# A gathered mixture of experts: 1280 dense and 768 gathered value columns from two table copies, sums in PSUM, 256 low parts on GpSimd

## The chip, the cores and the metric

The kernel runs on one core of one Trainium2 chip. The metric is the device time of one execution in microseconds. An execution has five engines that work side by side: TensorE (PE, with its weight loads as PEld), VectorE (DVE), ScalarE (ACT), GpSimd (POOL) and SyncE (SP, which here only issues transfers). Each runs its own instructions in order and waits for the others by semaphores.

## The reference, cut to what matters

The program is one decoder block over 256 tokens of width 2048. Its last part, which the change is about, is a mixture of experts: each token picks 16 of 16384 experts in each of 8 heads, weighs them, and sums their rows of the value table.

```python
def peer_ffn(y, wq, sub_keys, u_tab, v_tab):
    ...
        u = u_tab[eidx]                                   # 256 tokens, 8 heads, 16 experts, 2048 columns
        v = v_tab[eidx]
        h = jax.nn.gelu(jnp.einsum('btd,bthkd->bthk', yb, u))
        return jnp.einsum('bthk,bthkd->btd', g * h, v).astype(y.dtype)
...
        ffn = peer_ffn(x, peer_wq[l], peer_keys[l], peer_u[l], peer_v[l])
        x = layer_norm(DN_ALPHA * x + ffn, ln2_g[l], ln2_b[l])
```

Both tables have 16384 rows of 2048 columns in float32.

## The kernel before, in words

The program runs in stages: input projections, attention and convolution, output projection and the first layer norm, then the U stage (a score for each token and expert, about 425 to 870 us), a stage that turns scores into weights, the V stage (about 1080 to 1575 us), and the second layer norm. The change is in the V stage, in what leads into it and in the last norm.

The V stage sums the value rows in two ways, by column. For the columns from `GC` = 640 on (`VC` = 1408 of them) the sum is dense: the 16384 rows are taken in 128 steps of 128 rows, and in each step TensorE multiplies the weights `W` of both halves of the tokens (tt 0 and 1, 128 tokens each) with the 128 rows. For the first 640 columns it is gathered: token p of half tt has 128 chosen experts; in step j GpSimd issues an indirect transfer that brings the row of the j-th choice of each token, and VectorE adds it, times its weight `wv`, to `gacc`.

TensorE multiplies in three products per block, since one pass rounds: `mm3` takes high part times high part (L296), high times low (L297) and low times high (L298). ACT rounds the 128 x 1408 tile `vr` to its high part `vh` (L1785), VectorE subtracts to get the low part `vl` (L1786), and so for the weights, `wh` and `wl`, for two steps at once (L1774, L1775). The 1408 columns are three blocks of 512, 512 and 384, so a step has 18 matmuls: three blocks, two halves, three products. Their sums stay in six PSUM tiles (`f`) from the first step to the last.

The order is written out by hand, with no scheduler. In step j the loop issues the load and the gathers of step j+2 (`v_load`: SP for `vr`, POOL for `gv`), splits the rows of step j+1 (`v_split`), adds the gathered rows of step j (`v_gather`), and multiplies step j (`v_use`). `vr` has three buffers, `gv` has `GVB` = 7, and `vh` and `vl` have one in each of two pools that alternate, so the split of step j+1 overwrites what the matmuls of step j-1 read. Nine of the 256 gathers, the entries of `AHEAD`, are made before the stage begins: ACT scales them by their weight (L1799) and GpSimd adds them to `gacc` (L1802), between other work; 247 sums over 125 steps are left (L1750). The last three steps have no gathers. Step 0's split is made ahead too, by GpSimd.

In the U stage the same kinds of work appear: the dense table rows come from a copy that the host lays out contiguously (`u_dense`), GpSimd issues gathers `gu` (L1168), VectorE's dot products read a token row `yp` that lies in PSUM (L1179), and the low part `ul` is shared between VectorE (L1237) and GpSimd (L1238). The `hp` matmuls there (L1515, L1516, L1519) have 256 columns. In the projections L257 makes low parts of 512 columns on VectorE and GpSimd after one ACT instruction.

After step 127 the second layer norm runs block by block: `L2066` adds the residual `z` of half 1 by a matmul, `L2104` that of half 0 on VectorE, then statistics (L2097), `center` (L2089) and `shift` (L2093) on VectorE; one block of half 0 and the gathered columns of both halves go over ACT (L2083) and GpSimd (L2084, L2085).

Of the kernel before, what the change touches and what calls it, by code (L numbers as in the profile page):

```python
# [1 line left out]

# [6 lines left out]
F32 = mybir.dt.float32  # L9
# [4 lines left out]
AF = mybir.ActivationFunctionType  # L14
OP = mybir.AluOpType
# [4 lines left out]
P = 128  # L20
# [14 lines left out]
BIG = 1.0e33  # L35
GC = 640
AHEAD = (*range(9, 100, 12), 126)
LATER = {9: (125, 0), 33: (126, 1), 45: (127, 0), 69: (125, 1), 93: (127, 1)}
GVB = 7
UG = 896  # L40
# [6 lines left out]
VC = D - GC  # L47
# [32 lines left out]
def tile_hybrid_block(  # L80
    ctx: ExitStack,
    tc: tile.TileContext,
    x, w_in, pos_k, w1_k, w2_k, pos_v, w1_v, w2_v, dw_w, dw_b, cln_g, cln_b,
    w_out, ln1_g, ln1_b, wq, keys, u_dense, u_rows, v_tab, ln2_g, ln2_b, out,
    dbg=None, stop=None,
):
    nc = tc.nc
    x, w_in, w_out, wq = x[0], w_in[0], w_out[0], wq[0]
    v_tab, out = v_tab[0], out[0]
    dbg = dbg or {}  # L90
# [1646 lines left out]
    def v_raw(j):  # L1737
        raws[j] = vr_.tile([P, VC], F32, name=f"vr{j}", tag="vr", bufs=3)
        nc.sync.dma_start(raws[j], v_tab[j * P:(j + 1) * P, GC:])

    gvs = {}

    def v_fetch(j, tt):
        gvs[j, tt] = vr_.tile([P, GC], F32, name=f"gv{j}_{tt}", tag="gv", bufs=GVB)
        nc.gpsimd.indirect_dma_start(  # L1745
            out=gvs[j, tt], out_offset=None, in_=v_tab,
            in_offset=bass.IndirectOffsetOnAxis(ap=fl(e4, tt)[:, j:j + 1], axis=0))

    def v_sum(j, tt, engine):
        engine.scalar_tensor_tensor(gacc[:, tt], gvs.pop((j, tt)), wv[:, tt, j:j + 1], gacc[:, tt],  # L1750
                                    op0=OP.mult, op1=OP.add)
# [25 lines left out]
    def v_cols(j, s, early=False):  # L1777
# [6 lines left out]
        else:  # L1784
            nc.scalar.activation(vh, src[:, s], AF.Copy)  # L1785
        (nc.gpsimd if early else nc.vector).tensor_tensor(vl, src[:, s], vh.bitcast(F32), op=OP.subtract)  # L1786

# [195 lines left out]
    if stop == "u":  # L1983
        dump("hv", hv)
        if "H" in dbg:
# [5 lines left out]
    vps.append(vp_)  # L1991
    acc = [[psv_.tile([P, 512], F32, name=f"f{tt}{b}", tag=f"f{tt}{b}")[:, :e - a]
            for b, (a, e) in enumerate(blocks)]
           for tt in range(2)]

    def v_gather(j):
# [3 lines left out]
    def v_part(j, tt, b, stop=False):  # L2000
        (wh, wl), vhl = halves_[j // 2], parts[j]
        (a, e), s = blocks[b], slice(tt * P, tt * P + P)
        mm3(acc[tt][b], wh[:, s, j % 2], wl[:, s, j % 2], vhl[0][:, a:e], vhl[1][:, a:e], j == 0, stop)

# [14 lines left out]
    z2 = []  # L2019
    if True:  # L2020
        v_rows(0, 1)
        for j in range(P):
# [3 lines left out]
            if j == 0:  # L2026
                pass
            elif j + 2 < P:
# [22 lines left out]
            if j == P - 3:  # L2051
                for tt in range(2):
                    for i in range(2):
                        nc.vector.bn_stats(stat[:, tt, nb + i], gacc[:, tt, i * GC // 2:(i + 1) * GC // 2])
            if j == 0:
# [6 lines left out]

        for tt in range(2):
            if tt:
                for b, (a, e) in enumerate(blocks):
                    nc.tensor.matmul(acc[tt][b], lhsT=scaled, rhs=z2[tt][:, a:e], start=False, stop=False)  # L2066
            for j in (P - 2, P - 1):
                for b in range(nb):
                    v_part(j, tt, b, j == P - 1)
        zb = [acc[tt] + [gacc[:, tt]] for tt in range(2)]  # L2070
        zs = [[z2[tt][:, a:e] for a, e in blocks] + [gacc[:, tt]] for tt in range(2)]
# [60 lines left out]
        "dw_w", "dw_b", "conv_ln_g", "conv_ln_b", "w_out", "ln1_g", "ln1_b",  # L2132
        "peer_wq", "peer_keys", "peer_u_dense", "peer_u_rows", "peer_v", "ln2_g", "ln2_b"]
_OUTS = [((1, T, D), "float32")]
# [27 lines left out]
```

## Time and profile before

| what | value |
|---|---|
| median of 3 runs | 1589.48 us (1586.29 to 1589.81) |
| the profiled execution | 1588.19 us, its span 1586.4 us |
| busy: PE, DVE, ACT, POOL | 1550.8, 1367.0, 899.4, 1044.3 us |
| granted TensorE clock | 0.993 |
| bytes read from HBM | 459.80 MB, 293 GB/s over the span |

A group's row reads: line, engine, operation, the tile written `<-` the tiles read, the shape written `<-` the shape read, how many; then busy microseconds and mean nanoseconds of one; then the engine's idle time just before them and what ended most of it. A row of the timeline begins with its start and its length in microseconds, and `xN` marks merged instructions. A row of the windows gives each engine's busy time, the granted clock, the mean busy share of the 16 DMA engines and the GB/s that they moved. A row of the DMA queues gives packets, MB and the share of time that the packets took; q1 carries SP's loads, q0 GpSimd's gathers. Matmuls are pipelined and overlap, so the distance between two starts tells what one costs, not its length.

### The profile page before, as it was taken

The page shows a single profiled execution, that of the slowest core. Times are in us where ns is not written, and L with a number is a line of the kernel's source. Part 1 is how long each engine was busy: PE and PEld are TensorE (multiplying, and loading weights), DVE is VectorE, ACT ScalarE, POOL GpSimd, SP SyncE. Part 2 cuts the span into 40 slices and gives each one's busy share as a digit, 9 for nine tenths or more (in the row PEclk, how much of TensorE's full clock was granted, in tenths as well). Part 3 has the DMA queues.
Part 4 walks back from the last instruction along what each step waited for, and adds up shares of the span by engine and source line. Part 5 has one row for each costly group of instructions (what it writes and reads, how often), then busy time and mean ns, then how long its engine had stood idle before and what let it go on. Part 6 is the DMA issues. An engine that isn't in the chain of part 4 may idle for free.

```text
span 1586.4 us, 29450 instructions
## 1 busy us (share of the span) xinstructions
PE 1550.8 (98%) x10987; PEld 1435.9 (91%) x10987; DVE 1367.0 (86%) x2509; ACT 899.4 (57%) x1266; POOL 1044.3 (66%) x791
## 2 busy tenths in 40 slices
PE   9999999999999999999998999999999999999997
PEld 9999999988999999999998977788888888888886
DVE  6999777766578999999997788888999989989998
ACT  5345776645435777777776656785444444444443
POOL 1886000064887777777776677867888878878883
PEclk9999999999999999999999999999999999999999
DMA  9774455255867999999999886767999999999997
GB/s 299 239 231 147 139 161 184 92 207 182 258 209 272 397 382 393 383 390 384 387 388 366 304 276 216 235 196 247 346 368 355 356 371 346 357 376 355 366 356 248
DMA packets 161896, 466.59 MB, mean 294 GB/s; under 512 B 18304, under 2 KB 86424, under 8 KB 161496
## 3 DMA queue, kind: packets, MB, share of 16 engines
q1 hardware_dynamic: 117188, 261.95, 47.8%
q0 software_dynamic: 41040, 201.82, 34.5%
q8 instruction: 86, 1.41, 0.4%
q10 hardware_dynamic: 3524, 0.95, 0.3%
q14 instruction: 58, 0.48, 0.1%
HBM read 459.80 MB, written 4.85 MB: 293 GB/s over the span
## 4 chain that ended last, share of the span: by engine, by line
PE 83%; DVE 7%; DMA 3%; POOL 3%; issue 2%; ACT 2%; POOLq 0%; ACTq 0%; DVEq 0%
PE f L297 10%; PE f L298 10%; PE f L296 10%; PE hp L1515 8%; PE hp L1516 8%; PE hp L1519 7%; PE bank L1722 3%; DVE taps L492 2%; PE pwq L298 2%; PE pwq L297 2%; PE pwq L296 2%; PE bank L1674 2%; DMA feat<-fr 1%; PE mixa L296 1%; PE pcg L297 1%
## 5 line engine op out<-in xcount | busy, mean ns | idle before, releaser
L1745 POOL DMA_INDIRECT gv<-in_peer_v_dram,e x256 | 400.5, 1565 | 91.1 <-DVE gacc L1750 48.3
L1785 ACT ACTIVATE vh<-vr 128x1408 fp32r<-128x1408 f32 (+1 forms) x129 | 175.8, 1364 | 274.8 <-DVE gacc L1750 230.9
L297 PE MATMUL f<-vl,wh 128*128 128x512 f32 (+1 forms) x768 | 288.3, 375 | 1.7 <-DVE vl L1786 1.7
L296 PE MATMUL f<-vh,wh 128*128 128x512 f32 (+1 forms) x768 | 288.5, 376 | 0.0
L298 PE MATMUL f<-vh,wl 128*128 128x512 f32 (+1 forms) x768 | 288.1, 375 | 0.0
L1515 PE MATMUL hp<-yh,uh 128*128 128x256 f32 x1152 | 283.8, 285 | 4.2 <-ACT W L1522 4.2
L1516 PE MATMUL hp<-yl,uh 128*128 128x256 f32 x1152 | 283.4, 284 | 0.0
L257 POOL TENSOR_TENSOR lo<-raw,hi 128x1024 fp32r<-128x1024 f32 (+1 forms) x84 | 189.0, 2271 | 133.9 <-ACT hi L239 127.8
L1168 POOL DMA_INDIRECT gu<-in_peer_u_rows_dram,e x200 | 193.6, 968 | 117.9 <-DVE gu L1179 72.0
L1786 DVE TENSOR_TENSOR vl<-vr,vh 128x1408 fp32r<-128x1408 f32 (+1 forms) x129 | 206.5, 1602 | 41.3 <-ACT vh L1785 39.9
L1515 PEld LDWEIGHTS hp<-yh,uh 128*128 128x128 f32 x1152 | 222.5, 193 | 4.8 <-ACT W L1522 4.8
L1516 PEld LDWEIGHTS hp<-yl,uh 128*128 128x128 f32 x1152 | 222.6, 193 | 0.0
L1179 DVE SCALAR_TENSOR_TENSOR gu<-gu,yp 128x896 f32<-128x896 f32 x200 | 211.2, 1080 | 12.2 <-DMA gu<-in_peer_u_rows_dram,e 12.2
L239 ACT ACTIVATE hi<-raw 128x1024 fp32r<-128x1024 f32 (+1 forms) x137 | 141.2, 1036 | 141.0 <-PE pcg L297 29.1
L1750 DVE SCALAR_TENSOR_TENSOR gacc<-gv,hv,gacc 128x640 f32<-128x640 f32 x247 | 207.4, 880 | 2.9 <-DMA gv<-in_peer_v_dram,e 2.8
L1232 ACT ACTIVATE uh<-ur 128x1152 fp32r<-128x1152 f32 x128 | 149.6, 1168 | 95.6 <-issue 69.3
L297 PEld LDWEIGHTS f<-vl,wh 128*128 128x128 f32 x768 | 148.8, 194 | 22.9 <-DVE vl L1786 2.4
L296 PEld LDWEIGHTS f<-vh,wh 128*128 128x128 f32 x768 | 148.8, 194 | 20.7
L298 PEld LDWEIGHTS f<-vh,wl 128*128 128x128 f32 x768 | 149.0, 194 | 19.5
L1519 PE MATMUL hp<-yh,ul 128*128 128x256 f32 x1152 | 159.3, 284 | 0.0
L1519 PEld LDWEIGHTS hp<-yh,ul 128*128 128x128 f32 x1152 | 147.6, 192 | 0.1
L1237 DVE TENSOR_TENSOR ul<-ut,uh 128x768 fp32r<-128x768 f32 x126 | 119.9, 952 | 26.1 <-ACT ut L1236 23.2
(407 smaller groups left out, 3491.6 us busy)
## 6 DMA issues: line engine op xcount, KB each, us to landing
vr<-in_peer_v_dram SPq DMA_DIRECT2D x128, 704.0 KB
ur<-in_peer_u_dense_dram SPq DMA_DIRECT2D x128, 576.0 KB
raw<-in_w_in_dram SPq DMA_DIRECT2D x32, 1024.0 KB
raw<-in_w_out_dram SPq DMA_DIRECT2D x16, 1024.0 KB
raw<-in_peer_wq_dram SPq DMA_DIRECT2D x15, 1024.0 KB
gv<-in_peer_v_dram,e POOLq DMA_INDIRECT x256, 7.4
gu<-in_peer_u_rows_dram,e POOLq DMA_INDIRECT x200, 6.5
raw<-in_w_in_dram SPq DMA_DIRECT2D x4, 608.0 KB
```

Source lines behind the costliest of these rows:

```text
L257: e.tensor_tensor(lo[:, a:b], src[:, a:b], hi[:, a:b].bitcast(F32), op=OP.subtract)
L296: nc.tensor.matmul(acc, lhsT=ah, rhs=bh, start=start, stop=False)
L297: nc.tensor.matmul(acc, lhsT=ah, rhs=bl, start=False, stop=False)
L298: nc.tensor.matmul(acc, lhsT=al, rhs=bh, start=False, stop=stop)
L1168: nc.gpsimd.indirect_dma_start(out=gt, out_offset=None, in_=u_rows, in_offset=bass.IndirectOffsetOnAxis(ap=fl(e4, tt)[:, c:c + 1], axis=0))
L1179: nc.vector.scalar_tensor_tensor(gt, gt, 1.0, yr, op0=OP.mult, op1=OP.mult, accum_out=hv[:, tt, c:c + 1])
L1515: nc.tensor.matmul(hps[j], lhsT=uh[:, s], rhs=chunk(yh, k), start=k == 0, stop=False)
L1516: nc.tensor.matmul(hps[j], lhsT=uh[:, s], rhs=chunk(yl, k), start=False, stop=False)
L1519: nc.tensor.matmul(hps[j], lhsT=ul[:, s], rhs=chunk(yh, k), start=False, stop=k == UK - 1)
L1745: nc.gpsimd.indirect_dma_start(out=gvs[j, tt], out_offset=None, in_=v_tab, in_offset=bass.IndirectOffsetOnAxis(ap=fl(e4, tt)[:, j:j + 1], ...
L1750: engine.scalar_tensor_tensor(gacc[:, tt], gvs.pop((j, tt)), wv[:, tt, j:j + 1], gacc[:, tt], op0=OP.mult, op1=OP.add)
L1786: (nc.gpsimd if early else nc.vector).tensor_tensor(vl, src[:, s], vh.bitcast(F32), op=OP.subtract)
```

## The change

`GC` becomes 768 and so `VC` 1280: blocks of 512, 512 and 256. The host hands over two copies of the value table, `v_dense` with the last 1280 columns and `v_rows_` with the first 768, each contiguous. The gathered sums go to `pg`, a PSUM tile of three banks, to which ACT copies `gacc` ahead of the split for step 1; the two 256-column accumulators share one bank, `fboth`. For a whole step VectorE makes the low part of 1024 columns and GpSimd that of the other 256. The gather ring has six buffers and, from the second gather of step 3 on, two more in another pool for every fourth gather. The last multiplications come in another order, so that the shared bank is done before the last two blocks of half 1. Lines after the change are two or more further down: L298 to L300 are the three products, L1749 the gather, L1754 the sum, L1789 and L1794 the high and low parts.

```diff
@@ -1,4 +1,5 @@
 from contextlib import ExitStack
+from itertools import count
 
 import concourse.bass as bass
 import concourse.tile as tile
@@ -33,10 +34,11 @@
 ALPHA = 2.0 ** 0.25
 NEG = -3.0e38
 BIG = 1.0e33
-GC = 640
+GC = 768
 AHEAD = (*range(9, 100, 12), 126)
 LATER = {9: (125, 0), 33: (126, 1), 45: (127, 0), 69: (125, 1), 93: (127, 1)}
-GVB = 7
+GVB = 6
+GVX = 2
 UG = 896
 UD = D - UG
 UK = UD // P
@@ -81,12 +83,12 @@
     ctx: ExitStack,
     tc: tile.TileContext,
     x, w_in, pos_k, w1_k, w2_k, pos_v, w1_v, w2_v, dw_w, dw_b, cln_g, cln_b,
-    w_out, ln1_g, ln1_b, wq, keys, u_dense, u_rows, v_tab, ln2_g, ln2_b, out,
+    w_out, ln1_g, ln1_b, wq, keys, u_dense, u_rows, v_dense, v_rows_, ln2_g, ln2_b, out,
     dbg=None, stop=None,
 ):
     nc = tc.nc
     x, w_in, w_out, wq = x[0], w_in[0], w_out[0], wq[0]
-    v_tab, out = v_tab[0], out[0]
+    out = out[0]
     dbg = dbg or {}
 
     def dump(name, ap):
@@ -1736,18 +1738,20 @@
 
     def v_raw(j):
         raws[j] = vr_.tile([P, VC], F32, name=f"vr{j}", tag="vr", bufs=3)
-        nc.sync.dma_start(raws[j], v_tab[j * P:(j + 1) * P, GC:])
-
-    gvs = {}
+        nc.sync.dma_start(raws[j], v_dense[j * P:(j + 1) * P])
+
+    gvs, gv_turns = {}, count()
 
     def v_fetch(j, tt):
-        gvs[j, tt] = vr_.tile([P, GC], F32, name=f"gv{j}_{tt}", tag="gv", bufs=GVB)
+        turn = next(gv_turns) if len(vps) > 1 else 0
+        pool, bufs = (vps[1], GVX) if turn % (GVB // GVX + 1) == 1 else (vr_, GVB)
+        gvs[j, tt] = pool.tile([P, GC], F32, name=f"gv{j}_{tt}", tag="gv", bufs=bufs)
         nc.gpsimd.indirect_dma_start(
-            out=gvs[j, tt], out_offset=None, in_=v_tab,
+            out=gvs[j, tt], out_offset=None, in_=v_rows_,
             in_offset=bass.IndirectOffsetOnAxis(ap=fl(e4, tt)[:, j:j + 1], axis=0))
 
     def v_sum(j, tt, engine):
-        engine.scalar_tensor_tensor(gacc[:, tt], gvs.pop((j, tt)), wv[:, tt, j:j + 1], gacc[:, tt],
+        engine.scalar_tensor_tensor(pg[:, tt], gvs.pop((j, tt)), wv[:, tt, j:j + 1], pg[:, tt],
                                     op0=OP.mult, op1=OP.add)
 
     def v_rest(j):
@@ -1783,7 +1787,11 @@
             nc.gpsimd.tensor_copy(vh, src[:, s])
         else:
             nc.scalar.activation(vh, src[:, s], AF.Copy)
-        (nc.gpsimd if early else nc.vector).tensor_tensor(vl, src[:, s], vh.bitcast(F32), op=OP.subtract)
+        whole = s == slice(0, VC)
+        for e, c in ((nc.vector, slice(0, 1024)), (nc.gpsimd, slice(1024, VC))) if whole else \
+                ((nc.gpsimd if early else nc.vector, s),):
+            vh, vl = (t[:, c] for t in vhl)
+            e.tensor_tensor(vl, src[:, c], vh.bitcast(F32), op=OP.subtract)
 
     def v_split(j):
         if j % 2 == 0:
@@ -1989,9 +1997,12 @@
     psv_ = psv.enter_context(tc.tile_pool(name="psv", bufs=1, space=PSUM, reuse_waits="tile"))
     vp_ = psv.enter_context(tc.tile_pool(name="vp1", bufs=1, reuse_waits="tile", side="right"))
     vps.append(vp_)
-    acc = [[psv_.tile([P, 512], F32, name=f"f{tt}{b}", tag=f"f{tt}{b}")[:, :e - a]
-            for b, (a, e) in enumerate(blocks)]
+    acc = [[psv_.tile([P, 512], F32, name=f"f{tt}{b}", tag=f"f{tt}{b}") for b in range(nb - 1)]
            for tt in range(2)]
+    both = flat3(psv_.tile([P, 512], F32, name="fboth", tag="fboth"), 2, VC - blocks[-1][0])
+    for tt in range(2):
+        acc[tt].append(both[:, tt])
+    pg = psv_.tile([P, 2, GC], F32, name="pg", tag="pg")
 
     def v_gather(j):
         for pair in v_rest(j):
@@ -2000,7 +2011,8 @@
     def v_part(j, tt, b, stop=False):
         (wh, wl), vhl = halves_[j // 2], parts[j]
         (a, e), s = blocks[b], slice(tt * P, tt * P + P)
-        mm3(acc[tt][b], wh[:, s, j % 2], wl[:, s, j % 2], vhl[0][:, a:e], vhl[1][:, a:e], j == 0, stop)
+        mm3(acc[tt][b], wh[:, s, j % 2], wl[:, s, j % 2], vhl[0][:, a:e], vhl[1][:, a:e],
+            j == 0 and not (tt and b == nb - 1), stop)
 
     def v_use(j, tts=range(2)):
         for b in range(nb):
@@ -2024,7 +2036,8 @@
                 v_split(2)
                 v_gather(0)
             if j == 0:
-                pass
+                for tt in range(2):
+                    nc.scalar.activation(pg[:, tt], gacc[:, tt], AF.Copy)
             elif j + 2 < P:
                 v_load(j + 2)
             elif len(z2) < 2:
@@ -2051,7 +2064,7 @@
             if j == P - 3:
                 for tt in range(2):
                     for i in range(2):
-                        nc.vector.bn_stats(stat[:, tt, nb + i], gacc[:, tt, i * GC // 2:(i + 1) * GC // 2])
+                        nc.vector.bn_stats(stat[:, tt, nb + i], pg[:, tt, i * GC // 2:(i + 1) * GC // 2])
             if j == 0:
                 v_use(j, (0,))
                 v_use(j, (1,))
@@ -2060,14 +2073,22 @@
         for b, (a, e) in enumerate(blocks):
             nc.sync.dma_start(bcol[b], ln2_b[:, GC + a:GC + e].to_broadcast([P, e - a]))
 
-        for tt in range(2):
-            if tt:
-                for b, (a, e) in enumerate(blocks):
-                    nc.tensor.matmul(acc[tt][b], lhsT=scaled, rhs=z2[tt][:, a:e], start=False, stop=False)
-            for j in (P - 2, P - 1):
-                for b in range(nb):
-                    v_part(j, tt, b, j == P - 1)
-        zb = [acc[tt] + [gacc[:, tt]] for tt in range(2)]
+        def residual(b):
+            a, e = blocks[b]
+            nc.tensor.matmul(acc[1][b], lhsT=scaled, rhs=z2[1][:, a:e], start=False, stop=False)
+
+        for j in (P - 2, P - 1):
+            for b in range(nb):
+                v_part(j, 0, b, j == P - 1 and b < nb - 1)
+        residual(nb - 1)
+        for j in (P - 2, P - 1):
+            v_part(j, 1, nb - 1, j == P - 1)
+        for b in range(nb - 1):
+            residual(b)
+        for j in (P - 2, P - 1):
+            for b in range(nb - 1):
+                v_part(j, 1, b, j == P - 1)
+        zb = [acc[tt] + [pg[:, tt]] for tt in range(2)]
         zs = [[z2[tt][:, a:e] for a, e in blocks] + [gacc[:, tt]] for tt in range(2)]
 
 
@@ -2130,7 +2151,7 @@
 
 _INS = ["x", "w_in", "cmp_pos_k", "cmp_w1_k", "cmp_w2_k", "cmp_pos_v", "cmp_w1_v", "cmp_w2_v",
         "dw_w", "dw_b", "conv_ln_g", "conv_ln_b", "w_out", "ln1_g", "ln1_b",
-        "peer_wq", "peer_keys", "peer_u_dense", "peer_u_rows", "peer_v", "ln2_g", "ln2_b"]
+        "peer_wq", "peer_keys", "peer_u_dense", "peer_u_rows", "peer_v_dense", "peer_v_rows", "ln2_g", "ln2_b"]
 _OUTS = [((1, T, D), "float32")]
 
 
@@ -2147,6 +2168,8 @@
     u = inputs["peer_u"][0]
     inputs["peer_u_dense"] = u[:, :UD].reshape(P, P, UK, P).transpose(0, 3, 2, 1).reshape(P * P, UD)
     inputs["peer_u_rows"] = u[:, UD:]
+    v = inputs["peer_v"][0]
+    inputs["peer_v_dense"], inputs["peer_v_rows"] = v[:, GC:], v[:, :GC]
     for name in _INS:
         a = _np.ascontiguousarray(inputs[name])
         arrays[f"in_{name}_dram"] = a
```

VectorE's queue in two steps of the V stage, before and after. `hv` is the name that the tile of the weights `wv` bears there.

```order
L1775 TENSOR_TENSOR wl_17024<-W,wh_17023 128x512 [waits PE_49,Activation_49]
L1786 TENSOR_TENSOR vl_17028<-vr_16987,vh_17027 128x1408 [waits DMAHW5_49,Activation_49]
L1750 SCALAR_TENSOR_TENSOR gacc<-gv_0_16955,hv,gacc 128x640 [waits DMASW5_49,DVE_49]
L1750 SCALAR_TENSOR_TENSOR gacc<-gv_1_16957,hv,gacc 128x640 [waits DMASW6_49,DVE_49]
L1786 TENSOR_TENSOR vl_17058<-vr_17017,vh_17057 128x1408 [waits DMAHW6_49,Activation_49]
```

```order
L1779 TENSOR_TENSOR wl_17075<-W,wh_17074 128x512 [waits PE_49,Activation_49]
L1794 TENSOR_TENSOR vl_17079<-vr_17037,vh_17078 128x1024 [waits DMAHW3_49,Activation_49]
L1754 SCALAR_TENSOR_TENSOR pg<-gv_0_17004,hv,pg 128x768 [waits DMASW1_49,DVE_49]
L1754 SCALAR_TENSOR_TENSOR pg<-gv_1_17006,hv,pg 128x768 [waits DMASW2_49,DVE_49]
L1794 TENSOR_TENSOR vl_17110<-vr_17068,vh_17109 128x1024 [waits DMAHW4_49,Activation_49]
```

The order is the same; the low part is 384 columns shorter, the sums are 128 wider, and they read and write `pg`.

GpSimd's queue in the same stage, before and after (the waits name the ring of transfers, DMASW, and the engine that frees a buffer; `e` holds the row numbers).

```order
L1745 DMA gv_0_16861<-in_peer_v_dram,e_4315 128x640 [waits DMASW0_49,DVE_49]
L1745 DMA gv_1_16863<-in_peer_v_dram,e_4315 128x640 [waits DMASW1_49,DVE_49]
L1745 DMA gv_0_16891<-in_peer_v_dram,e_4315 128x640 [waits DMASW2_49,DVE_49]
L1745 DMA gv_1_16893<-in_peer_v_dram,e_4315 128x640 [waits DMASW3_49,DVE_49]
L1745 DMA gv_0_16925<-in_peer_v_dram,e_4315 128x640 [waits DMASW4_49,DVE_49]
```

```order
L1794 TENSOR_TENSOR vl_16846<-vr_16804,vh_16845 128x256 [waits DMAHW4_49,Activation_49]
L1749 DMA gv_0_16872<-in_peer_v_rows_dram,e_4315 128x768 [waits DMASW1_49,DVE_49]
L1749 DMA gv_1_16874<-in_peer_v_rows_dram,e_4315 128x768 [waits DMASW2_49,DVE_49]
L1794 TENSOR_TENSOR vl_16881<-vr_16839,vh_16880 128x256 [waits DMAHW5_49,Activation_49]
L1749 DMA gv_0_16907<-in_peer_v_rows_dram,e_4315 128x768 [waits DMASW3_49,DVE_49]
L1749 DMA gv_1_16909<-in_peer_v_rows_dram,e_4315 128x768 [waits DMASW4_49,DVE_49]
L1794 TENSOR_TENSOR vl_16912<-vr_16870,vh_16911 128x256 [waits DMAHW6_49,Activation_49]
```

Between the gathers of step j+2 and those of j+3 now stands a subtraction that waits for ACT's high part of step j+1.

ACT's queue where the V stage begins, before and after.

```order
L1774 ACTIVATE wh_13228<-W 128x256 [waits DVE_49,Activation_49]
L1785 ACTIVATE vh_13352<-vr_12956 128x1408 [waits DMAHW6_49,DMAHW5_49,DMAHW7_49,DMAHW4_49,DMAHW2_49]
L1774 ACTIVATE wh_13374<-W 128x512 [waits DMAHW4_49,DMAHW5_49,DMAHW3_49,DMAHW6_49,DMAHW2_49,DMAHW7_49,DMAHW1_49,DMAHW0_49]
L1785 ACTIVATE vh_13378<-vr_13226 128x1408 [waits DMAHW2_49,PE_49,Pool_49]
L2050 ACTIVATE scaled<-ident 128x128
```

```order
L1778 ACTIVATE wh_13228<-W 128x256 [waits DVE_49,Activation_49]
L2040 ACTIVATE pg<-gacc 128x768 [waits PE_49,Pool_49]
L2040 ACTIVATE pg<-gacc 128x768 [waits Activation_49]
L1789 ACTIVATE vh_13354<-vr_12956 128x1280 [waits DMAHW6_49,DMAHW7_49,DMAHW5_49,DMAHW2_49]
L1778 ACTIVATE wh_13377<-W 128x512 [waits DMAHW6_49,DMAHW4_49,DMAHW7_49,DMAHW1_49,DMAHW0_49]
L1789 ACTIVATE vh_13381<-vr_13226 128x1280 [waits DMAHW2_49,PE_49]
L2063 ACTIVATE scaled<-ident 128x128
```

Two copies from `gacc` to `pg` have come in front of the high part for step 1; the first of them waits for GpSimd and for TensorE.

TensorE's last matmuls of a step and the first of the next, before and after.

```order
L296 MATMUL f_13340<-vh_16161,wh_16127 128x384
L297 MATMUL f_13340<-vl_16162,wh_16127 128x384
L298 MATMUL f_13340<-vh_16161,wl_16128 128x384
L296 MATMUL f_13343<-vh_16161,wh_16127 128x384
L297 MATMUL f_13343<-vl_16162,wh_16127 128x384
L298 MATMUL f_13343<-vh_16161,wl_16128 128x384
L296 MATMUL f_13338<-vh_16195,wh_16191 128x512 [waits Activation_49]
L297 MATMUL f_13338<-vl_16196,wh_16191 128x512 [waits DVE_49]
```

```order
L298 MATMUL fboth<-vh_13852,wh_13848 128x256
L299 MATMUL fboth<-vl_13853,wh_13848 128x256 [waits Pool_49]
L300 MATMUL fboth<-vh_13852,wl_13849 128x256
L298 MATMUL fboth<-vh_13852,wh_13848 128x256
L299 MATMUL fboth<-vl_13853,wh_13848 128x256
L300 MATMUL fboth<-vh_13852,wl_13849 128x256
L298 MATMUL f_13338<-vh_13883,wh_13848 128x512 [waits Activation_49]
L299 MATMUL f_13338<-vl_13884,wh_13848 128x512 [waits DVE_49]
```

The third block writes one bank for both halves, and its first high-times-low product waits for GpSimd.

## The prediction

> **What bounds the kernel now.** I read the page's chain first, then the groups by shape and one step of the timeline, to see what paces the V stage; then the windows and DMA queues, to see how much room the transfers have.
>
> ```profile
> span 1586.4 us, 29450 instructions
> PE 83%; DVE 7%; DMA 3%; POOL 3%; issue 2%; ACT 2%; POOLq 0%; ACTq 0%; DVEq 0%
> ...
> L297 PE MATMUL f<-vl,wh 128*128 128x512 f32 x512 | 202.2, 395 | 1.7 <-DVE vl L1786 1.7
> ```
> ```profile
> 1300.91 0.39 PE L296 MATMUL f<-vh,wh 128*128 128x512 f32 x1
> 1301.11 1.38 ACT L1785 ACTIVATE vh<-vr 128x1408 fp32r<-128x1408 f32 x1 [1.88 <-DVE gacc L1750]
> 1301.14 0.40 PE L297 MATMUL f<-vl,wh 128*128 128x512 f32 x1
> ...
> 1303.70 0.34 PE L296 MATMUL f<-vh,wh 128*128 128x384 f32 x1
> 1303.88 0.34 PE L297 MATMUL f<-vl,wh 128*128 128x384 f32 x1
> ...
> 1304.95 1.38 ACT L1785 ACTIVATE vh<-vr 128x1408 fp32r<-128x1408 f32 x1 [2.46 <-DVE gacc L1750]
> ```
> The chain is 83% TensorE. In the V stage (from about 1080 us to 1575) a step takes 3.84 us: two `vh` splits start at 1301.11 and 1304.95. TensorE's twelve 512-column matmuls take 1303.70 - 1300.91 = 2.79, 0.2325 each; six of 384 columns, started 0.17 to 0.18 apart, take the remaining 1.05. Nothing is left over, and TensorE's waits for `vl` in the whole stage are 1.7 us. The trace puts ACT's wait down to the gathered sum, but `vh` needs the buffer that the matmuls of two steps before read; step and sum end in the same 0.03 us, and the matmuls are the condition.
>
> **The matmuls.** They keep their number; the third block goes from 384 to 256 columns.
>
> ```profile
> 600.42 0.28 PE L1515 MATMUL hp<-yh,uh 128*128 128x256 f32 x1
> ...
> 600.54 0.28 PE L1516 MATMUL hp<-yl,uh 128*128 128x256 f32 x1
> ```
> At 256 columns this trace starts one every 0.12 us. A step becomes 2.79 + 6 x 0.12 = 3.51: 0.33 less, or 42 us over 128 steps. This is the most that the change can give.
>
> **VectorE.** It loses 384 of the low part's 1408 columns and gets sums of 768 columns for 640, with the accumulator in PSUM.
>
> ```profile
> 1298.68 1.63 DVE L1786 TENSOR_TENSOR vl<-vr,vh 128x1408 fp32r<-128x1408 f32 x1 [0.62 <-ACT vh L1785]
> ...
> 1300.22 1.68 DVE L1750 SCALAR_TENSOR_TENSOR gacc<-gv,hv,gacc 128x640 f32<-128x640 f32 x2
> ```
> ```profile
> L1750 DVE SCALAR_TENSOR_TENSOR gacc<-gv,hv,gacc 128x640 f32<-128x640 f32 x247 | 207.4, 880 | 2.9 <-DMA gv<-in_peer_v_dram,e 2.8
> L1786 DVE TENSOR_TENSOR vl<-vr,vh 128x1408 fp32r<-128x1408 f32 x126 | 204.8, 1625 | 41.3 <-ACT vh L1785 39.9
> L257 DVE TENSOR_TENSOR lo<-raw,hi 128x1024 fp32r<-128x1024 f32 x45 | 54.3, 1219 | 10.1 <-ACT hi L239 10.1
> L1775 DVE TENSOR_TENSOR wl<-W,wh 128x512 fp32r<-128x512 f32 x63 | 43.2, 687 | 0.0
> ...
> L2089 DVE SCALAR_TENSOR_TENSOR f<-f,mv,ln2g 128x512 f32<-128x512 f32 x4 | 3.0, 754 | 0.1
> ...
> L2104 DVE SCALAR_TENSOR_TENSOR f<-z,f 128x512 f32<-128x512 f32 x2 | 1.4, 696 | 0.2 <-PE f L298 0.2
> ```
> A low part of 1408 holds VectorE 1.54 us (1298.68 to 1300.22). Lengths grow by (1625 - 1219)/384 = 1.06 ns a column, so 1024 columns hold it 1.54 - 0.41 = 1.13. The sum's new form has no row; the nearest is L2104, which reads and writes PSUM: 696 ns at 512, so 696 + 256 x 1.06 = 967 ns at 768. The other end is L2089 with 754, giving 1025. I take L2104, as it has the same one operand in SBUF. With 247 sums over 125 steps (1.976 a step) and a `wl` every other step: 1.13 + 1.976 x 0.967 + 0.34 = 3.38, at the dear end 3.50. VectorE has 0.13 us left under TensorE's 3.51, or nothing: what covered it before (3.84) is mostly spent.
>
> **GpSimd.** It gets a subtraction of 256 columns for each step, in its queue between the gathers of step j+2 and those of j+3.
>
> ```profile
> L1745 POOL DMA_INDIRECT gv<-in_peer_v_dram,e x256 | 400.5, 1565 | 91.1 <-DVE gacc L1750 48.3 <-issue 40.4 <-DMA gv<-in_peer_v_dram,e 1.5
> L1168 POOL DMA_INDIRECT gu<-in_peer_u_rows_dram,e x200 | 193.6, 968 | 117.9 <-DVE gu L1179 72.0 <-issue 6.8 <-PE pwq L298 5.8
> ...
> L1786 POOL TENSOR_TENSOR vl<-vr,vh 128x512 fp32r<-128x512 f32 x2 | 2.5, 1274 | 0.2
> ...
> L1786 POOL TENSOR_TENSOR vl<-vr,vh 128x384 fp32r<-128x384 f32 x1 | 1.0, 1011 | 0.1
> ```
> The two rows of L1786 give 2.05 ns a column, so 256 cost 0.75. A gather occupies GpSimd 1565 ns in the V stage but 968 in the U stage, where VectorE's dot products read `yp` from PSUM. With the sums in PSUM I take 0.97 each; with the 0.30 us between two issues, 0.75 + 2 x (0.97 + 0.30) = 3.29, under 3.51. At 1565 it would be 4.48, but most of that is waiting for VectorE, which the sums in PSUM stop causing.
>
> The low part starts on the same signal as VectorE's. What that does stands in the earlier splits:
>
> ```profile
> 363.96 0.69 DVE L257 TENSOR_TENSOR lo<-raw,hi 128x512 fp32r<-128x512 f32 x1 [2.03 <-ACT hi L239]
> 364.00 1.79 POOL L257 TENSOR_TENSOR lo<-raw,hi 128x512 fp32r<-128x512 f32 x1 [0.93 <-ACT hi L239]
> ...
> 366.72 1.29 POOL L257 TENSOR_TENSOR lo<-raw,hi 128x512 fp32r<-128x512 f32 x1 [0.92 <-ACT hi L239]
> 367.23 1.32 DVE L257 TENSOR_TENSOR lo<-raw,hi 128x512 fp32r<-128x512 f32 x1
> ```
> Whoever starts first runs at its own length and the other waits: started together, VectorE is first by 0.04, takes 0.69, and GpSimd 1.79 for 1.29. In the V stage GpSimd then ends about 1.2 + 0.75 = 2.0 after `vh`. The gathers behind it go out later by that, and have three steps before their sums. TensorE waits for GpSimd only at the first L299 matmul into `fboth`, 12 x 0.23 = 2.8 into the step, some 3 us after GpSimd is done. The load of `vr` now waits for both low parts, about 0.8 later; it has three steps less 1.3 (ACT's split), 1.2 and 0.8, so 7.2 us.
>
> ```profile
> L1785 ACT ACTIVATE vh<-vr 128x1408 fp32r<-128x1408 f32 x126 | 174.2, 1383 | 272.3 <-DVE gacc L1750 230.9 <-PE f L298 30.9 <-DMA vr<-in_peer_v_dram 9.7
> ```
> With 8.5 us for it (three steps of 3.84 less 1.4 and 1.6), ACT waited for `vr` 9.7 us in all, so a little may show. I put GpSimd's subtraction at 0 per step; if GpSimd starts first, VectorE pays up to 0.75.
>
> **The transfers.** A step moved 704 KB of dense rows and 1.976 x 320 KB of gathered ones, 1.368 MB; now 640 and 1.976 x 384, 1.432 MB. In 3.51 us that is 408 GB/s.
>
> ```profile
> core 0: us, PE busy (x) PEld busy (x) DVE busy (x) ACT busy (x) POOL busy (x), PEclk, DMA share, GB/s
> 515.00:555.00 40.00, 40.00 (x336) 40.00 (x335) 39.40 (x85) 29.96 (x37) 30.81 (x31) 1.00 1.01 397
> ...
> 840.00:850.00 10.00, 10.00 (x85) 10.00 (x85) 8.61 (x17) 6.95 (x9) 7.36 (x8) 1.00 1.03 413
> ...
> 1460.00:1500.00 40.00, 40.00 (x189) 35.06 (x188) 36.80 (x37) 17.16 (x16) 33.60 (x22) 1.00 0.97 359
> ```
> ```profile
> q1 hardware_dynamic: 14429, 72.25, 53.9%
> q0 software_dynamic: 15612, 63.95, 44.0%
> ...
> q0 software_dynamic: 11060, 63.45, 52.3%
> q1 hardware_dynamic: 13747, 56.31, 47.5%
> ```
> The V stage moves 359 GB/s with engines busy 0.97 of the time, the U stage 397 at 1.01 over 40 us and 413 over 10, still with TensorE fully busy. So a share near 1 isn't the limit by itself. The queue rows (first pair 1180 to 1560 us, second 520 to 830) give MB by busy time: the strided dense rows ran at 72.25/(0.539 x 380) = 353 GB/s, the dense copy of the U table at 56.31/(0.475 x 310) = 382; gathers 382 and 391. The new dense copy should move from the first figure toward the second. At 413 GB/s a step costs 3.47 and TensorE paces; at the U stage's rates of both queues, 387 together, 3.70; at the present 359, 3.99. I take 400, just above the best 40 us, because in the U stage nothing asked for more: 1.432/0.400 = 3.58.
>
> The Trainium skill, "DMA: Bandwidth & Descriptors", section Specifications, gives about 358 GB/s as the HBM limit of one core. By it a step would take 4.00 and the kernel would be slower by 20 us and the fixed costs. The 397 above does not agree with it.
>
> **Start and end.** ACT copies the two accumulators to PSUM ahead of `vh` of step 1, and waits there for GpSimd's last ahead sum, which is 9 x 0.28 us later less what the smaller third column block saves.
>
> ```profile
> 1077.46 1.54 POOL L1802 TENSOR_TENSOR gacc<-gacc,gv 128x640 f32<-128x640 f32 x1
> ...
> 1081.14 1.36 ACT L1785 ACTIVATE vh<-vr 128x1408 fp32r<-128x1408 f32 x1
> ...
> 1580.01 1.53 POOL L2084 TENSOR_TENSOR gacc<-gacc,ln2b 128x640 f32<-128x640 f32 x1
> ...
> 1581.63 1.53 POOL L2085 TENSOR_TENSOR gacc<-gacc,ln2b 128x640 f32<-128x640 f32 x1
> ```
> The sum ends at about 1081 for 1079; two copies of 0.84 put `vh` at 1082.7 for 1081.1, and a step that is 0.3 shorter hides none of it: 1.7 us. At the end two GpSimd operations of 768 for 640 add 2 x 0.27, ACT's 0.1, and VectorE gets the shared bank later by some 0.4: 1.0 us.
>
> **Sum**, on the profiled execution, 1588.2 us (span 1586.4, 1.8 around it): 125 steps x (3.84 - 3.58) = 32.5, three last steps without gathers x 0.33 = 1, less 2.7: 1588.2 - 30.8 = 1557.4. The median of the runs lies 1.3 above the profiled one, so I predict 1559.
>
> **Rivals.**
> TensorE paces: the transfers reach 408 GB/s. For it speak 413 over 10 us and VectorE's 3.38; against, that no 40 us held it. a step of 3.51 gives 1550.
> Partly held up: transfers at the U stage's 387, or VectorE at 3.50 with no room for a single wait, make a step of 3.68 to 3.80: 1571 to 1586.
> GpSimd first (slower): its low part starts while VectorE ends `wl` or a sum, and `vl` waits up to 0.75. It decides from a mean stall of 0.46 a step, where 3.38 reaches 3.84; at the full 0.75 a step is 4.13, 36 us more, and the time 1628. For it speaks 367.23; against, that GpSimd comes out of its gathers late and then waits for `vl` itself.
> The transfers stay at 359 GB/s (slower): a step of 3.99 gives 1610. For it speaks 0.97 at 359; against it the U stage. This is what the page's limit would do.
> Lost in the middle: a step of about 3.82, no change.
>
> **The numbers.** With step s the time is 1591.2 - 125 x (3.84 - s). Forecast 0.53 (steps of 3.53 to 3.68, 1552 to 1571), TensorE paces 0.20, partly held up 0.12, GpSimd first 0.05, transfers at 359 0.06, no change 0.04. The three first make 0.85 for faster; slower 0.11; the same, within 0.2% or 3 us, about what the runs' spread can tell, 0.04. The range runs from the bound by TensorE, 1547 with 3 us for the start, to a step of 3.75, 1580; outside lie the slower cases, the unchanged one and half of the third.
>
> **What would show it.** Starts of `vh` 3.5 to 3.65 apart; 390 to 405 GB/s in the V windows; gathers near 1.0 us on GpSimd; sums near 0.97 and some 0.1 to 0.2 us a step of VectorE waiting for `gv` or ACT for `vr`; GpSimd's subtraction at about 1.9, with no TensorE wait for it; TensorE idle about 2 us after step 0. Wrong if `vl` lengthens well over 1.2, if the V windows stay under 370 GB/s, or if a sum costs over 1.05.

## The result and the profile after

The changed kernel takes 1572.07 us (median of four runs, 1570.83 to 1576.62) beside 1589.64 for the kernel before: a ratio of 0.9898, 95% interval 0.9882 to 0.9913. That is 17.6 us less where 30.6 were forecast; the time lies in the range, 1 us inside the third case (1571 to 1586). One execution of 5292 us, of the kernel with the layout alone (below), is left out of its ratio. First the page's span and chain of the changed kernel, then 340 us of the V stage in one window, before and after (columns as in the prediction's windows: busy us of PE, PEld, DVE, ACT and POOL, granted clock, DMA share, GB/s).

```profile
span 1569.6 us, 29840 instructions
...
PE 52%; DMA 17%; DVE 11%; POOL 8%; issue 8%; ACT 4%; POOLq 0%; ACTq 0%; DVEq 0%; SPq 0%
DMA vr<-in_peer_v_dense_dram 10%; PE hp L1517 7%; PE hp L1518 7%; PE hp L1521 7%; DMA gv<-in_peer_v_rows_dram,e 4%; DVE pg L1754 3%; POOL gv L1749 3%; DVE taps L494 2%; POOL vl L1794 2%; PE pwq L300 2%; PE pwq L299 2%; PE bank L1676 2%; PE pwq L298 2%; PE bank L1724 2%; PE mixa L298 1%
```
```profile
1180.00:1520.00 340.00, 340.00 (x1596) 298.15 (x1595) 310.35 (x309) 146.66 (x133) 280.20 (x176) 1.00 0.99 361
```
```profile
1180.00:1520.00 340.00, 335.29 (x1671) 283.50 (x1670) 318.21 (x323) 144.51 (x139) 296.16 (x277) 1.00 1.01 394
```

TensorE's share of the chain has fallen from 83% to 52%; 17% are now transfers, most of them the dense load `vr`. The windows say the same from the other side: 394 GB/s where the stage before moved 361, and TensorE busy 335.29 of 340. The groups of the changed kernel in this window, and what ACT waits for from 1140 to 1540 us (total us, times, longest):

```profile
L1749 POOL DMA_INDIRECT gv<-in_peer_v_rows_dram,e x184 | 211.3, 1148 | 42.0 <-issue 19.4 <-DVE pg L1754 16.1 <-DMA vr<-in_peer_v_dense_dram 1.1
L1754 DVE SCALAR_TENSOR_TENSOR pg<-gv,hv,pg 128x768 f32<-128x768 f32 x184 | 187.5, 1019 | 3.2
...
L1794 DVE TENSOR_TENSOR vl<-vr,vh 128x1024 fp32r<-128x1024 f32 x93 | 115.6, 1243 | 18.6 <-ACT vh L1789 17.2
L1794 POOL TENSOR_TENSOR vl<-vr,vh 128x256 fp32r<-128x256 f32 x93 | 85.5, 920 | 2.0 <-ACT vh L1789 0.4
```
```profile
ACT vh L1789 <- DMA vr<-in_peer_v_dense_dram: 170.5, 81, 3.3
```

In the kernel before, the wait for `vr` came to 9.7 us; now it ends ACT's idle time 81 times in 400 us. To see what that does to the steps I took the 120 gaps between starts of `vh` from the trace, from the fifth on. Before: mean 3.855, median 3.840, four gaps over 4.1 us. After: mean 3.679, median 3.560, sixteen over 4.1. A late split does not always hold TensorE up, so I took TensorE's own steps too, from first matmul to first matmul, between 1110 and 1530 us: their median is 3.547, 77 of 114 stay under 3.7, and what the 114 take beyond 3.547 adds up to 15.0 us. So two steps in three run at TensorE's own pace, and a third come late. One late round, in the timeline:

```profile
1272.88 1.27 ACT L1789 ACTIVATE vh<-vr 128x1280 fp32r<-128x1280 f32 x1 [1.40 <-DMA vr<-in_peer_v_dense_dram]
...
1274.67 1.22 DVE L1794 TENSOR_TENSOR vl<-vr,vh 128x1024 fp32r<-128x1024 f32 x1
1275.18 1.53 POOL L1749 DMA_INDIRECT gv<-in_peer_v_rows_dram,e  x1 [0.30 <-issue]
...
1276.73 0.75 POOL L1794 TENSOR_TENSOR vl<-vr,vh 128x256 fp32r<-128x256 f32 x1
...
1284.27 1.28 ACT L1789 ACTIVATE vh<-vr 128x1280 fp32r<-128x1280 f32 x1 [2.85 <-DMA vr<-in_peer_v_dense_dram]
```
```profile
1277.51 0.33 SPq L1741 DMA_DIRECT2D vr<-in_peer_v_dense_dram  x1
```

VectorE is done with the buffer of `vr` at 1275.89. GpSimd still issues a gather, which stands ahead in its queue and takes 1.53 us beside VectorE's subtraction, and ends its own 256 columns at 1277.48. Only then is the next load into this buffer issued (1277.51), and the split that needs it starts 6.76 us later, after waiting 2.85 us for it. Three steps have taken 11.39 us, 3.80 each.

By stage, from the two traces: `vh` of step 1 starts 4.03 us later (1085.17 for 1081.14), the next 125 steps take 22.1 us less, and the rest from there to the end takes 1.3 us more. Together -16.8, the difference of the spans.

### The profile page after: what moved, and what is told of

It is laid out like the page before. It is cut to its first block, busy times and chain, and to the rows that moved or that the text cites. A ratio compares the mean times of both kernels' runs of the same rounds, so it can differ in the third digit from the quotient of the medians.

```text
span 1569.6 us, 29840 instructions
## 1 busy us (share of the span) xinstructions
PE 1523.6 (97%) x10987; PEld 1397.0 (89%) x10987; DVE 1361.5 (87%) x2509; ACT 888.0 (57%) x1268; POOL 1056.8 (67%) x917
## 4 chain that ended last, share of the span: by engine, by line
PE 52%; DMA 17%; DVE 11%; POOL 8%; issue 8%; ACT 4%; POOLq 0%; ACTq 0%; DVEq 0%; SPq 0%
DMA vr<-in_peer_v_dense_dram 10%; PE hp L1517 7%; PE hp L1518 7%; PE hp L1521 7%; DMA gv<-in_peer_v_rows_dram,e 4%; DVE pg L1754 3%; POOL gv L1749 3%; DVE taps L494 2%; POOL vl L1794 2%; PE pwq L300 2%; PE pwq L299 2%; PE bank L1676 2%; PE pwq L298 2%; PE bank L1724 2%; PE mixa L298 1%
## 5 line engine op out<-in xcount | busy, mean ns | idle before, releaser
L1749 POOL DMA_INDIRECT gv<-in_peer_v_rows_dram,e x256 | 290.5, 1135 | 63.7 <-issue 29.9
L1789 ACT ACTIVATE vh<-vr 128x1280 fp32r<-128x1280 f32 (+1 forms) x129 | 162.2, 1259 | 265.9 <-DMA vr<-in_peer_v_dense_dram 189.9
L1754 DVE SCALAR_TENSOR_TENSOR pg<-gv,hv,pg 128x768 f32<-128x768 f32 x247 | 251.7, 1019 | 4.3
L299 PE MATMUL f<-vl,wh 128*128 128x512 f32 x512 | 208.3, 407 | 9.0 <-DVE vl L1794 8.3
L298 PE MATMUL f<-vh,wh 128*128 128x512 f32 x512 | 203.5, 397 | 0.6 <-ACT vh L1789 0.6
L300 PE MATMUL f<-vh,wl 128*128 128x512 f32 x512 | 202.6, 396 | 0.0
L1794 DVE TENSOR_TENSOR vl<-vr,vh 128x1024 fp32r<-128x1024 f32 (+1 forms) x129 | 160.5, 1245 | 25.6 <-ACT vh L1789 23.8
L1240 POOL TENSOR_TENSOR ul<-ur,uh 128x384 fp32r<-128x384 f32 x128 | 132.7, 1037 | 8.4 <-ACT uh L1234 6.0
L299 PEld LDWEIGHTS f<-vl,wh 128*128 128x128 f32 x512 | 99.6, 195 | 39.0 <-DVE vl L1794 22.7
L1794 POOL TENSOR_TENSOR vl<-vr,vh 128x256 fp32r<-128x256 f32 (+1 forms) x129 | 122.8, 952 | 9.3 <-ACT vh L1789 7.0
```

The source lines that it names most:

```text
L298: nc.tensor.matmul(acc, lhsT=ah, rhs=bh, start=start, stop=False)
L299: nc.tensor.matmul(acc, lhsT=ah, rhs=bl, start=False, stop=False)
L300: nc.tensor.matmul(acc, lhsT=al, rhs=bh, start=False, stop=stop)
L1749: nc.gpsimd.indirect_dma_start(out=gvs[j, tt], out_offset=None, in_=v_rows_, in_offset=bass.IndirectOffsetOnAxis(ap=fl(e4, tt)[:, j:j + 1] ...
L1754: engine.scalar_tensor_tensor(pg[:, tt], gvs.pop((j, tt)), wv[:, tt, j:j + 1], pg[:, tt], op0=OP.mult, op1=OP.add)
L1794: e.tensor_tensor(vl, src[:, c], vh.bitcast(F32), op=OP.subtract)
```

## Experiments

Theories: the rate of the transfers paces; VectorE has no room and paces; the round of the three `vr` buffers (held by both low parts, then reloaded) paces. Ratios are to the kernel before on the same chip, with 95% intervals; the changed kernel has 0.9898. Gaps are the 120 described above.

**Half the gathered bytes.** L1749 and the sum:

```diff
-            out=gvs[j, tt], out_offset=None, in_=v_rows_,
+            out=gvs[j, tt][:, :GC // 2] if len(vps) > 1 else gvs[j, tt], out_offset=None, in_=v_rows_,
...
-        engine.scalar_tensor_tensor(pg[:, tt], gvs.pop((j, tt)), wv[:, tt, j:j + 1], pg[:, tt],
+        half = gvs.pop((j, tt))[:, :GC // 2].rearrange("p (o j) -> p o j", o=1).to_broadcast([P, 2, GC // 2])
+        engine.scalar_tensor_tensor(flat3(pg[:, tt], 2, GC // 2), half, wv[:, tt, j:j + 1], ...
```

> The changed kernel, but from step 1 on each gather brings 384 of its 768 columns, and the sum reads these twice: half the gathered bytes, the same instructions and lengths on every engine. The output is not the layer's. If the transfers pace the step (1.43 MB at about 393 GB/s make 3.65 us), 1.04 MB leave TensorE's own 3.54: 125 x 0.13 less, about 1556. If VectorE with its sums of 1.02 to 1.04 us paces, nothing moves: 1572. If the round of the three vr buffers paces, landing gets shorter too, and it also gives about 1556.

Measured 1555.34 us, ratio 0.978 (0.9758 to 0.9802). The same window of this run:

```profile
1180.00:1520.00 340.00, 340.00 (x1727) 294.83 (x1726) 328.59 (x334) 149.92 (x144) 294.01 (x285) 1.00 0.88 297
```

TensorE is busy throughout; gaps: mean 3.551, median 3.547, none over 4.1. So VectorE and GpSimd, with all their instructions and waits on each other, do keep up with 3.55, and what is lost in the changed kernel is lost through the transfers. The run doesn't say whether by their rate or by their landing: the load of `vr` lands 4.5 us after its issue here, 6.2 in the changed kernel (medians over 116 steps, to the last row packet of each load).

**The layout undone.** Tables strided as before:

```diff
-        nc.sync.dma_start(raws[j], v_dense[j * P:(j + 1) * P])
+        nc.sync.dma_start(raws[j], v_tab[j * P:(j + 1) * P, GC:])
...
-            out=gvs[j, tt], out_offset=None, in_=v_rows_,
+            out=gvs[j, tt], out_offset=None, in_=v_tab,
```

> The changed kernel reading one table of 2048 columns, as before: dense rows are 5120 of every 8192 bytes, gathered ones 3072 of 8192. If the transfers pace, the old rates (353 GB/s dense, 382 gathered) make 1.432 MB last 3.89 us, a step longer by 0.22: about 1600. If VectorE or TensorE paces, or if the layout has no part in the rate: 1572.

Measured 1575.70 us, ratio 0.9905 (0.9884 to 0.9927), almost the interval of the changed kernel. The queue rows of 1180 to 1520 us, first of the changed kernel, then of this one:

```profile
q1 hardware_dynamic: 13519, 61.57, 46.8%
```
```profile
q1 hardware_dynamic: 13389, 60.94, 46.3%
```

61.57/(0.468 x 340) and 60.94/(0.463 x 340) are both 387 GB/s. The strided rows move as fast as the dense ones once the queues are kept full.

**The layout alone,** in the kernel before (the same lines the other way):

> The kernel before with nothing but the table in two dense copies (640 gathered columns, 1408 dense). TensorE paces it at 3.84 with the transfers at 359 GB/s, so no change: 1589.5 within 3. The prediction's rates would show in the trace: dense rows at 382 GB/s of busy time instead of 353, and a share of about 0.94 instead of 0.98. If the layout has no part in the rates: 353 and 0.98 as before.

Measured ratio 1.0003 (0.9992 to 1.0014). The row of the dense queue in the same 340 us gives 64.53/(0.520 x 340) = 365 GB/s, 353 in the kernel before, and the window a share of 0.98 for 0.99. The dense rows' busy rate moves a little, the time doesn't:

```profile
q1 hardware_dynamic: 12892, 64.53, 52.0%
```

**The sums in SBUF.**

```diff
-    pg = psv_.tile([P, 2, GC], F32, name="pg", tag="pg")
+    pg = gacc
...
-                for tt in range(2):
-                    nc.scalar.activation(pg[:, tt], gacc[:, tt], AF.Copy)
+                pass
```

> The changed kernel with the gathered sums in SBUF as before (accumulator gacc, no copies to PSUM). If the place of the accumulator is what lets the gathers out, each gather waits again for VectorE (1.57 us and more against 1.15), GpSimd needs 0.75 + 2 x 1.9 = 4.5 a step at worst, and the time lies between 1600 and 1670. If it does not matter: 1572, less 1.6 for the copies that fall away.

Measured 1653.94 us, ratio 1.0393 (1.0353 to 1.0433); gaps: mean 4.39.

```profile
L1749 POOL DMA_INDIRECT gv<-in_peer_v_rows_dram,e x155 | 216.0, 1393 | 35.5 <-DVE gacc L1754 15.5 <-issue 12.6 <-DVE vl L1794 4.0
L1754 DVE SCALAR_TENSOR_TENSOR gacc<-gv,hv,gacc 128x768 f32<-128x768 f32 x156 | 177.8, 1177 | 0.1
```
```profile
PEld fboth L299 <- POOL vl L1794: 52.9, 55, 1.9
```

A gather holds GpSimd 1393 ns for 1148, a sum holds VectorE 1177 for 1019, and now TensorE waits for GpSimd's low part: 52.9 us of weight loads in 340. The accumulator in PSUM is what makes the rest of the change pay; without it the kernel is 4% slower than before.

**The low part back on VectorE.**

```diff
-        for e, c in ((nc.vector, slice(0, 1024)), (nc.gpsimd, slice(1024, VC))) if whole else \
...
+        (nc.gpsimd if early else nc.vector).tensor_tensor(vl, src[:, s], vh.bitcast(F32), op=OP.subtract)
```

> The changed kernel with the whole low part of 1280 columns on VectorE, as before; GpSimd only gathers. VectorE then needs about 1.41 + 1.976 x 1.03 + 0.34 = 3.79 a step. If the transfers pace now, VectorE takes over at 3.79: 1572 + 125 x 0.12 = 1587. If VectorE paces now, all 0.28 are added: 3.95, 1607. If late vr loads pace (GpSimd's low part holds their buffer), that part falls away, and it ends between 1572 and 1587.

Measured 1577.07 us, ratio 0.9912 (0.9887 to 0.9936). The time lies where late loads were expected to leave it, and in the 340 us window ACT's wait for `vr` falls from 148.0 to 79.4 us while VectorE's work rises from 318.21 to 330.97. What the earlier release gains may go into VectorE's longer work; this run doesn't separate the two, and the gain of GpSimd's share isn't shown here. 15 gaps are still over 4.1, at a median of 3.624. My 3.79 for VectorE was too much; a cleaner row of its need comes below.

**The round of the load buffers.** Four kernels. In the first GpSimd's low part stands between its two gathers:

```diff
-                v_load(j + 2)
+                v_raw(j + 2)
+                for pair in v_rest(j + 2)[:1]:
+                    v_fetch(*pair)
...
                 v_split(j + 1)
+            if 0 < j < P - 2:
+                for pair in v_rest(j + 2)[1:]:
+                    v_fetch(*pair)
```

> The changed kernel with GpSimd's low part between the two gathers of its step instead of behind both: the buffer of vr is free some 0.8 us earlier, and the next load is issued that much earlier. If the rate of the transfers paces (393 GB/s whatever is issued when), nothing moves: 1572 within 3. If the round of three vr buffers paces (about 3.9 us from a split to the next load's issue, 6.2 for it to land, together 10.1 of the three steps' 11.0, with tails), a step falls by 0.1 to 0.13: 1556 to 1560.

Measured 1579.04 us, ratio 0.9922 (0.9893 to 0.9952), runs from 1566 to 1584. The run doesn't decide: the edit hardly did what it was made for. From the start of a split to the issue of the load that reuses its buffer the mean is 3.54 us for 3.63 (over 117 steps), and a tenth of them still take 4.3 or more, as in the changed kernel.

In the second, the copies to PSUM stand behind the high parts of steps 1 and 2:

```diff
                 v_split(2)
+                for tt in range(2):
+                    nc.scalar.activation(pg[:, tt], gacc[:, tt], AF.Copy)
                 v_gather(0)
```

> The changed kernel with the two copies of the accumulators to PSUM behind the high parts of steps 1 and 2 on ScalarE instead of ahead of them: 1.65 us of them were ahead of step 1's high part. If the start counts for the end, 1.6 less: 1570.4. If the transfers of the first steps make up for it, 1572.

Measured 1572.16 us, ratio 0.988 (0.9858 to 0.9901). In the profiled runs the fifth split after the start begins at 1095.16 for 1099.42, 4.3 us earlier, and the one 120 steps on at 1541.17 for 1540.93: the lead is gone by then. Only some 1.6 of the lead are the edit's; this run was 2.7 ahead already at `wl`, before the copies (1067.98 for 1070.69). A single pair of runs, but it fits a stage whose loads set the pace.

Then six gather buffers for 6 + 2, and in the space of the two a fourth buffer for `vr`:

```diff
-        raws[j] = vr_.tile([P, VC], F32, name=f"vr{j}", tag="vr", bufs=3)
+        pool, bufs = (vps[1], 1) if j % 4 == 3 else (vr_, 3)
+        raws[j] = pool.tile([P, VC], F32, name=f"vr{j}", tag="vr", bufs=bufs)
...
-        turn = next(gv_turns) if len(vps) > 1 else 0
-        pool, bufs = (vps[1], GVX) if turn % (GVB // GVX + 1) == 1 else (vr_, GVB)
-        gvs[j, tt] = pool.tile([P, GC], F32, name=f"gv{j}_{tt}", tag="gv", bufs=bufs)
+        gvs[j, tt] = vr_.tile([P, GC], F32, name=f"gv{j}_{tt}", tag="gv", bufs=GVB)
```

> The changed kernel with six gather buffers instead of 6 + 2: gather n waits for sum n-6. Landing takes 7.0 us and a step has two gathers, so six are three steps, 11 us, ahead. If the rate of the transfers paces, it needs only enough requests outstanding: 1572 within 3. If the eight are needed to keep the queues full, the gathers come late and VectorE waits for gv: 0.1 a step or more, 1585 and above.

> As the kernel with six gather buffers, and the space of the other two holds a fourth buffer for vr. If the rate of the transfers paces: as with three, 1572 within 3, with the late steps a little rarer. If the round of three vr buffers paces, a step falls to TensorE's 3.55: 1556 to 1558.

Six gathers and three loads: 1582.88 us, ratio 0.9955 (0.9935 to 0.9975). Six gathers and four loads: 1561.69 us, ratio 0.981 (0.9786 to 0.9834). The fourth load buffer alone is worth 21 us. With three loads, the two gather buffers less cost some 9 us beside the changed kernel's 0.9898; the loads are then issued 4.0 us after the split for 3.6 and land as before (6.1, means), but why fewer gather buffers delay them isn't shown. The windows of the first and of the second, and the wait for `vr` in each:

```profile
1180.00:1520.00 340.00, 332.79 (x1652) 280.49 (x1651) 314.03 (x320) 141.60 (x136) 284.85 (x273) 1.00 1.00 388
```
```profile
1180.00:1520.00 340.00, 337.47 (x1705) 290.73 (x1705) 322.76 (x329) 147.11 (x142) 287.83 (x282) 1.00 1.02 402
```
```profile
ACT vh L1787 <- DMA vr<-in_peer_v_dense_dram: 142.8, 67, 4.3
```
```profile
ACT vh L1788 <- DMA vr<-in_peer_v_dense_dram: 8.0, 4, 2.4
```

The wait falls from 142.8 us to 8.0, the gaps from a mean of 3.751 with 26 over 4.1 to 3.601 with six, and the rate rises from 388 to 402 GB/s (394 in the changed kernel) with the same bytes a step. So 394 was not all that the transfers can do, and three load buffers are shown as the cause of most late steps. The loads did not get quicker by it: with four, they are issued 4.4 us after the split of the step whose buffer they take, for 4.0, and land in 6.5 for 6.1 (means). That makes 10.9, more than the 10.64 of three steps at 3.547; four steps have room for it. At 3.547 a step the stage asks for 1.432/3.547 = 404 GB/s, half a per cent above what it then gets. Whether the transfers could do more, no run shows.

**More on this base.** One gather buffer more (`GVX = 1`), the same with the copies later, and six gathers with the low part on VectorE:

> Four vr buffers and seven gather buffers (6 + 1): one gather buffer more than the kernel with four loads, whose VectorE waited 10.9 us for gathered rows. If these waits count: up to 4 us less than its 1561.7, so 1557 to 1561. If only the loads count: 1561.7 within 3.

> As the one with four loads and seven gathers, and the two copies to PSUM behind the high parts of steps 1 and 2. With three load buffers this brought nothing, since the loads paced the steps that follow. If TensorE paces most steps with four, the 1.65 us at the start now show: 1.6 less than the other. If the loads still pace: the same time.

> Four vr buffers, six gather buffers, and the whole low part on VectorE, with GpSimd left to gather. This shows what GpSimd's share is worth once late loads are rare. The prediction's lengths give VectorE 3.79 a step: 1562 + 125 x 0.19 = 1585. The run with three load buffers had VectorE busy 39.6 of 40 us at its undisturbed step of 3.62: then 1562 + 125 x 0.04 = 1567. If the share is worth nothing: 1562.

Ratios 0.9805 (0.9788 to 0.9822), 0.9801 (0.9786 to 0.9815) and 0.9885 (0.987 to 0.99). Neither the seventh gather buffer nor the later copies show beyond four loads. GpSimd's share does: without it the ratio is 0.75% higher, 12 us. VectorE is then the pace:

```profile
L1753 DVE SCALAR_TENSOR_TENSOR pg<-gv,hv,pg 128x768 f32<-128x768 f32 x184 | 187.6, 1020 | 3.2
L1789 DVE TENSOR_TENSOR vl<-vr,vh 128x1280 fp32r<-128x1280 f32 x94 | 139.6, 1485 | 0.4 <-ACT vh L1788 0.4
```

It sits idle 3.6 us in 340 before these two, the gaps have a mean of 3.663 and none over 4.1. This is VectorE's need with 1280 columns; 256 fewer are 1485 - 1243 = 242 ns less, so 3.42 for the changed kernel.

The best versions, with four loads, stand at 0.980 to 0.981, about 9 parts in 1000 faster than the changed kernel and 19 or 20 than the kernel before. Four loads beside eight gather buffers were not run.

## Why the prediction was right in sign and too large in size

The kernel got faster, as forecast, but by 17.6 us of the 30.6. That the number lies just inside the third case is luck: neither of that case's two causes was at work. The transfers are not held to 387 GB/s (402 with four loads), and VectorE needs 3.42 a step, not 3.50.

- **TensorE, 3.51.** The median of undisturbed gaps is 3.547: the 512-column matmuls start 0.234 to 0.235 apart, not 0.2325. The 0.04 a step put the bound by TensorE 5 us too low.
- **VectorE, 3.38 with 3.50 as dear end.** Measured 3.42; the sum in PSUM at 768 columns takes 1019 ns, between the 967 I took and the 1025 I named as the other end. Right, and the rival that VectorE holds the step up fell with the halved gathers.
- **GpSimd, gathers at 0.97, low part at no cost.** A gather takes 1148 on average: the one that starts beside VectorE's low part still takes 1.53 (1275.18 above). GpSimd first, as a stall of `vl`, did not come: VectorE's 1024 columns take 1.24 on average, 1.22 in the round above. GpSimd's subtraction takes 0.92 on average, not the 1.9 I expected; in the round above the gather before it is the one drawn out. But I let the subtraction end 2.0 us after the split; in the round above it ends 3.3 after it (1274.15 to 1277.48), because the gather ahead of it in the queue was left out of that working.
- **The load's slack, the step that failed.** From the late low part I left 7.2 us for a landing and wrote that "a little may show". From the start of a split to the next load into its buffer I had 1.3 + 1.2 + 0.8 = 3.3; measured are 3.6 as a mean and up to 4.8. The landing itself I never put beside the 7.2: it takes 6.1 (mean), 6.6 and more in one of twenty. And where a split waited for its load, it started another 1.3 us (median, at least 0.5) after the last row packet, for which I had nothing. Together 11.0, where three steps at TensorE's 3.547 have 10.64: the round doesn't fit, and three measured steps of 3.679 are 11.04. I had put nothing for it into the step. TensorE's late steps cost 15.0 us, where the forecast lacks 13, and with a fourth buffer most of them are gone.
- **Transfers, 3.58 at an even 400 GB/s.** The rate was about right (394, and 402 with four loads, where TensorE's steps ask for little more), the picture wrong: not every step at 3.58, but two in three at 3.55 and the others later. The reason that I gave, dense rows moving from 353 to 382, fell: layout by itself has no part in the time, and strided rows reach 387 too. The queue's rate by its busy time isn't what it can do; with half the gathers (and smaller packets on the other queue) the same dense rows come to 63.54/(0.576 x 340) = 324.

```profile
q1 hardware_dynamic: 13959, 63.54, 57.6%
```

- **Transfers held at 359 (slower).** Fell: 394 over 340 us, 402 with four loads. The limit of about 358 GB/s that the Trainium skill, "DMA: Bandwidth & Descriptors", section Specifications, gives for one core doesn't agree with these windows. The same page of the Trainium skill, section Bandwidth, has 425 GB/s for one core whose neighbour is idle, and about 358 for each when both stream. Only one core works here, and 394 and 402 lie between the two figures; no run here has a second core streaming.
- **Start 1.7, end 1.0.** The start came out at 4.0. The copies are 1.65 of it, as worked out. Of the rest 1.2 come from this place, where VectorE's `wl` took 1.73 us beside GpSimd's sum of 1.82 (0.42 in the kernel before); some 1.1 were there earlier and may be spread between runs: the run with half the gathers, the same up to here, has this split at 1081.85, 3.3 us earlier. The later copies suggest that little of it reaches the end. The tail after TensorE took 11.5 for 10.1 us, 1.5 more.

```profile
1070.30 1.82 POOL L1810 TENSOR_TENSOR gacc<-gacc,gv 128x768 f32<-128x768 f32 x1
...
1070.69 1.73 DVE L1779 TENSOR_TENSOR wl<-W,wh 128x256 fp32r<-128x256 f32 x1
```

What stays open is whether the issue or the landing makes more of the late steps. In the changed kernel the loads of late splits are issued 3.94 us after the split that held their buffer, 3.59 for the others, and land in 6.25 for 6.09; with six gather buffers it is 4.29 for 3.94 and 6.38 for 5.96 (means). So both have a part. Open too is what fills the half microsecond and more between a load's last packet and its split.

## What to carry to other kernels

When a change brings several resources to within a few per cent of the same step, the mean rate no longer tells the time: look at the spread, and give each buffer's round (from its first use to the issue of its reload, from there to landing, and on to the first use of what landed) its own sum against the steps that it has, with the tail of each. Follow the last of all the readers of a buffer, and count what stands ahead of it in its queue. Take a queue's capability from a stage that keeps it full, not from megabytes by busy time in a stage that doesn't.

## What the runs showed of the hardware

MB by busy time is no fixed rate of a queue: the same dense rows moved at 324 GB/s of busy time with half the gathers, where the stage moved 297 GB/s, and at 387 in the changed kernel, where it moved 394. A DMA share of 1.00 went with 388 GB/s, one of 1.02 with 402. Rows of 5120 bytes out of 8192 moved as fast as dense ones, both at 387. With the accumulator in PSUM in place of SBUF a sum took VectorE 1019 ns for 1177, and a gather took GpSimd 1148 for 1393.
